# Loading the queries and keys of an attention head: three transfers of 128 partitions in place of six of 64

## The chip, the cores and the metric

The kernel runs on one core of a Trainium2 chip. A core has TensorE (PE in the profile; PEld is its weight load), VectorE (DVE), ScalarE (ACT), GpSimd (POOL) and SyncE (SP), which here does nothing but issue transfers. Transfers are issued from three queues, those of SP, ACT and POOL, and carried by sixteen DMA engines which the three queues share. The metric is device microseconds of one execution. Before the change it is 2463.16 us, the median of three runs from 2460.84 to 2463.77.

## The reference

One layer of a decoder, 2048 tokens of width 1024, all in float32. The change touches the attention branch:

```python
hn = _rmsnorm(h, ln_mix[i]); z = hn @ w_in[i]
q, k, v = ...                       # 8 heads of 64 channels, q scaled by 1/8
att = _dilated_attention(q, k, v, slopes)     # three window/dilation patterns per head, mixed
h = h + concat([att, pool]) @ w_out[i]
# then a gated MLP with a causal convolution, a gated per-layer embedding, a final RMSNorm
```

A pattern with window w and dilation d lets token t attend to t, t-d, ..., t-w. The kernel computes two score tiles for a block of 128 queries, a "near" one (the dense window) and a "far" one (both dilated windows), each with its own bias table, maximum and sum.

## The kernel before, in words

Every float32 product is made of TensorE products on a number's high part (rounded to the format `float32r`) and its low part (the rest). Projections, for instance, are three matmuls (`mm3`, L88). Attention scores do this differently: the contraction over 64 channels would fill only half of the 128 partitions. So `load_qk` (L502) lays a head out with its two parts stacked. `ks` has the high part of the keys on partitions 0 to 63 and the low part on 64 to 127. `qhh` has the high part of the queries twice, on both halves, and `qll` their low part twice. One matmul of `qhh` with `ks` then gives high times high plus high times low, and one of `qll` with `ks` adds the rest.

The kernel goes through three phases:

- `phase_project` (L170) works in token chunks. For each it computes queries, keys, values and the pooling input, splits them, and stores the parts to DRAM: queries in `g.qh` and `g.ql`, keys in `g.kh` and `g.kl` (L376 and L377), one tensor for each pair of heads, 128 channels by 2048 tokens. Values go to `g.vn` and `g.vf` (L391), pooling results to `g.mh` and `g.ml` (L463, L464). In the last chunk keys come before values, and the values' stores are issued from POOL.
- `phase_attention` (L486) runs over 128 steps, 16 blocks of queries for each of 8 heads. The order of PE, ACT, DVE and POOL in a step is written out by hand in `CFG["ord"]`; the order on SP's queue is set by the planner that schedules the program. Head 0's transfers are issued before the first step. Those of head h+1 are put in a list at step 1 of head h and one is taken from it at each step; SP sends it as soon as its tile is free. The tiles of a head come in two sets, of even and odd heads (`tag=f"qhh{e}"`, `bufs=1`), so the loads of head h+1 must wait until head h-1 has finished its scores, and no longer. The two bias tables `fb` and `nb` follow in the same list. The values `v` of a pair of heads are loaded by eight transfers, at fixed steps (`V_STEPS`). Every second head the statistics of a pair go through DRAM (`std`, `stf` on ACT's queue, `wd` on POOL's), come back as weights spread over 128 partitions (`wb`, L891), and POOL mixes near and far results and stores them in `g.mh`, `g.ml` (L924, L925).
- `phase_rest` (L930) has the output projection, the MLP and the rest.

The transfer of L891 is used below. It reads two rows of 512 numbers and writes each of them to 64 partitions:

```python
q.dma_start(w, g.wd[pr][2 * a : 2 * a + 2, None, cs].to_broadcast([2, DH, CH]))
```

A transfer's source and destination are nested lists of sizes. For the loads of 64 partitions both begin with 64; for L891 the source begins with 2, the destination with 128.

Of the kernel before, what the change touches and what calls it, by code (L numbers as in the profile page):

```python
# [11 lines left out]
F32R = mybir.dt.float32r  # L12
# [5 lines left out]
P = 128  # L18
D = 1024
KD = D // P  # L20
S = 2048
H = 8
DH = 64
# [31 lines left out]
def rdma(nc, dst, src):  # L55
    nc.sync.dma_start(fp(dst) if dst.dtype == F32R else dst, fp(src) if src.dtype == F32R else src)
# [113 lines left out]
def phase_project(tc, g, xT, w_in, pool_w, rcnt):  # L170
# [4 lines left out]
    with ExitStack() as ctx:  # L175
# [116 lines left out]
        for c, (t0, n) in enumerate(chunks):  # L292
            cs = slice(t0, t0 + n)
            final = c == len(chunks) - 1
            nxt = None
            for gi, grp in enumerate((0, 1, 2, 3) if not final else (0, 1, 3, 2)):
                if gi == 2 and not final:
                    tk.later(2, lambda st=nxt: scale(st))
                    tk.later(5, lambda st=nxt: spread_(st))
                nt = 4 if grp != 2 else n // P  # L300
                ps = [psum.tile([P, CH], F32, tag="b1", name=f"z{c}_{grp}_{j}") for j in range(nt)]
                apart = final and grp == 2
                for k in range(KD if not apart else 0):
                    if gi == 0 and c == 0 and k < KD - ACFG["nk"]:
                        norm_b(cur, k + ACFG["nk"])
                        cur.low()
                    ahead(step + ACFG["la"])
                    step += 1
                    wh, wl = held[grp, k]
                    ah, al = cur.hn[k]  # L310
                    for j in range(nt):
                        js = slice(j * P, (j + 1) * P)
                        if grp == 2:
                            mm3(nc, ps[j], ah[:, js], al[:, js], wh, wl, k == 0, k == KD - 1)
                        else:
                            mm3(nc, ps[j][:, :n], wh[:, js], wl[:, js], ah, al, k == 0, k == KD - 1)
                    tk.tick()
                    if gi == 0 and k == 6 and not final:
                        nxt = loads(c + 1)
                    if gi == 1 and not final:  # L320
                        square(nxt, k)
                    if gi == 3 and not final:
                        if k > 1:
                            nxt.low()
                        norm_a(nxt, k)
                        if k > 0:
                            norm_b(nxt, k - 1)
                    if gi == 0 and c == 0:
                        if k < 4:
                            square(cur, 2 * k)  # L330
                            square(cur, 2 * k + 1)
                        if k == ACFG["sc"]:
                            scale(cur)
                        if k == KD - 1:
                            spread_(cur)
                            inv = nxt.xs[0][:, n : 2 * n]
                            nc.scalar.copy(inv, cur.inv)
                    if gi == 0 and c > 0 and k < 2:
                        cur.low()
                        if k == 0:  # L340
                            norm_b(cur, KD - 1)
                    if c == 0 and gi == 0 and k == 4:
                        raw = small("pw_raw")
                        nc.sync.dma_start(raw.rearrange("p (a b) -> p a b", a=4), pool_w)
                        split(nc, pw_h.rearrange("p a b -> p (a b)"), pw_l.rearrange("p a b -> p (a b)"), raw)
                        nc.sync.dma_start(rc, rcnt)
                unscaled = list(range(nt)) if c == 0 and grp != 2 else []

                def by_inv():
                    if unscaled:  # L350
                        pu = ps[unscaled.pop(0)][:, :n]
                        nc.vector.tensor_tensor(pu, pu, inv, op=ALU.mult)

                by_inv()
                for j in range(nt):
                    if apart:
                        for k in range(KD):
                            js = slice(j * P, (j + 1) * P)
                            ah, al = cur.hn[k]
                            mm3(nc, ps[j], ah[:, js], al[:, js], *held[grp, k], k == 0, k == KD - 1)  # L360
                            if k % 4 == 3:
                                tk.tick()
                    by_inv()
                    pj = ps[j][:, :n]
                    pr = pj.rearrange("p (j r) -> p r j", r=4)
                    if grp == 0:
                        hi, lo = zpair("q", n)
                        nc.scalar.activation(hi, pj, AF.Copy, scale=QSCALE)
                        nc.vector.scalar_tensor_tensor(lo, pj, QSCALE, fp(hi), op0=ALU.mult, op1=ALU.subtract)
                        rdma(nc, g.qh[j][:, cs], hi)  # L370
                        rdma(nc, g.ql[j][:, cs], lo)
                    elif grp == 1:
                        hi, lo = (by_residue(z) for z in zpair("k", n))
                        nc.scalar.copy(hi, pr)
                        nc.vector.tensor_tensor(lo, pr, fp(hi), op=ALU.subtract)
                        rdma(nc, residues(g.kh[j], t0, n), hi)  # L376
                        rdma(nc, residues(g.kl[j], t0, n), lo)  # L377
                    elif grp == 2:
                        vt = sb.tile([P, H, 2, DH], F32R, tag="vt", bufs=NV, name="vt")
                        pv = ps[j].rearrange("p (h d) -> p h d", h=H)  # L380
                        if c == 0:
                            sc = cur.pw[:, j : j + 1]
                            nc.scalar.activation(vt[:, :, 0, :], pv, AF.Copy, scale=sc)
                            nc.vector.scalar_tensor_tensor(
                                vt[:, :, 1, :], pv, sc, fp(vt[:, :, 0, :]), op0=ALU.mult, op1=ALU.subtract
                            )
                        else:
                            nc.scalar.copy(vt[:, :, 0, :], pv)
                            nc.vector.tensor_tensor(vt[:, :, 1, :], pv, fp(vt[:, :, 0, :]), op=ALU.subtract)
                        for dst in (g.vn[t0 // P + j], g.vf[:, t0 // P + j]):  # L390
                            (nc.gpsimd if final else nc.sync).dma_start(  # L391
                                fp(dst.rearrange("r j h a d -> j r (h a d)")), fp(vt.rearrange("p h a d -> p (h a d)"))
                            )
                    else:
                        pool_branch(nc, g, sb, psum1, c, j, pj, t0, n, tails[j], rc, pw_h, pw_l, zpair, final)
            cur = nxt
# [7 lines left out]
def residues(t, t0, n):  # L404

    c, j0 = t0 // CH, t0 % CH // 4
    return t[:, c, :, j0 : j0 + n // 4]
# [78 lines left out]
def phase_attention(tc, g, mx, near_b, far_b):  # L486
# [5 lines left out]
    with ExitStack() as ctx:  # L492
# [8 lines left out]
        def load_qk(h):  # L501
            t = heads[h] = Shared()  # L502
            pr, e = h // 2, h % 2
            rows = slice(DH * e, DH * e + DH)
            t.qhh = sb.tile([P, S], F32R, tag=f"qhh{e}", bufs=1, name=f"qhh{h}")
            t.qll = sb.tile([P, S], F32R, tag=f"qll{e}", bufs=1, name=f"qll{h}")
            t.qr = t.qhh.rearrange("p (c r) -> p r c", r=4)
            t.qlr = t.qll.rearrange("p (c r) -> p r c", r=4)
            t.ks = sb.tile([P, NCH, 4, P], F32R, tag=f"ks{e}", bufs=1, name=f"ks{h}")
            t.nb = sb.tile([P, 256], F32, tag=f"nb{e}", bufs=1, name=f"nb{h}")  # L510
            t.fb = sb.tile([P, 512], F32, tag=f"fb{e}", bufs=1, name=f"fb{h}")
            loads = []
            for half in range(2):
                hs = slice(half * DH, half * DH + DH)
                loads.append((t.qhh[hs], g.qh[pr][rows]))
                loads.append((t.ks[hs], (g.kh if half == 0 else g.kl)[pr][rows]))
                loads.append((t.qll[hs], g.ql[pr][rows]))
            loads += [(t.fb, far_b[h]), (t.nb, near_b[h])]
            return loads

        near_v = g.vn.rearrange("n r j (p h) a d -> (r j) n p (h a d)", h=2)
        far_v = g.vf.rearrange("r (b m) j (p h) a d -> r (m j) b p (h a d)", m=4, h=2)
# [1322 lines left out]
def tile_layer(ctx, tc, xT, pT, vec, w_in, pool_w, w_out, w_up, w_down, w_gate, w_ple, near_b, far_b, rcnt, outT, upto=9):  # L1845
# [23 lines left out]

    g.qh = per(NPAIR, [P, S], F32R, "qh")  # L1870
    g.ql = per(NPAIR, [P, S], F32R, "ql")
    g.kh = per(NPAIR, [P, NCH, 4, P], F32R, "kh")
    g.kl = per(NPAIR, [P, NCH, 4, P], F32R, "kl")

    g.vn = dr.tile([NQ, 4, P // 4, H, 2, DH], F32R, tag="vn", name="vn")
    g.vf = dr.tile([4, NQ, P // 4, H, 2, DH], F32R, tag="vf", name="vf")
# [95 lines left out]
```

## Time and profile before

| | |
|---|---|
| median of the runs | 2463.16 us |
| span of the profiled execution (its own time is not on the page) | 2454.4 us |
| what lies outside the span, if that execution took the median | 8.8 us |
| TensorE busy | 2345.7 us, 96% of the span |
| attention, from its first score matmul to its last | 397.7 to 706.4 us |
| transfers issued at L56 for `qhh` and `qll`, `ks` | 16 and 16, 16 |
| median time of one such transfer from issue to landing | 10.7, 14.1 and 12.0 us |

"Idle" behind a group of instructions is the time for which the engine stood still just before them, and the name behind the arrow is what ended it. Times to landing run from the issue to the last of a transfer's bytes, so they hold what is queued ahead of it. GB/s in a stretch of time is what all sixteen DMA engines moved together.

### The profile page before, as it was taken

How to read it: one execution, taken by the hardware profiler on the slowest of the kernel's cores; microseconds unless marked ns; L12 is line 12 of the kernel's file. 1: busy time of each engine (PE TensorE's matmuls, PEld its weight loads, DVE VectorE, ACT ScalarE, POOL GpSimd, SP SyncE). 2: the span in 40 equal slices, each digit the busy share in tenths (PEclk: the TensorE clock that was granted, in tenths of full speed). 3: DMA queues.
4: the chain of work that ended last, by engine and by line, in shares of the span. 5: the costliest groups of instructions: out<-in, count | busy, mean ns of one | idle time of the engine just before them, and what ended most of it. 6: DMA issues, size and time to landing. Idle time of an engine off the chain costs nothing.

```text
span 2454.4 us, 32544 instructions
## 1 busy us (share of the span) xinstructions
PE 2345.7 (96%) x11251; PEld 1970.6 (80%) x11251; DVE 1723.2 (70%) x2705; ACT 1146.1 (47%) x2055; POOL 547.3 (22%) x552
## 2 busy tenths in 40 slices
PE   8999999888879999999999999999999999999998
PEld 7888887787767887888888787788878888888888
DVE  6645437787774367999999989877766565755655
ACT  5423326787761125445445545444445444543332
POOL 3312221044340023344332366100020000000100
PEclk9999999898989999999999999999999999999999
DMA  7535448878747576456566778544388676654332
GB/s 240 175 133 185 146 153 249 178 173 193 181 142 260 189 253 202 161 187 211 192 197 219 260 275 272 197 145 142 125 287 287 226 255 206 215 176 158 125 100 91
DMA packets 248516, 476.06 MB, mean 194 GB/s; under 512 B 47744, under 2 KB 74176, under 8 KB 245280
## 3 DMA queue, kind: packets, MB, share of 16 engines
q1 hardware_dynamic: 199376, 385.20, 49.7%
q0 software_dynamic: 29328, 61.02, 7.4%
q10 hardware_dynamic: 19648, 27.77, 3.3%
q8 instruction: 88, 1.44, 0.3%
q14 instruction: 76, 0.62, 0.1%
HBM read 313.08 MB, written 160.73 MB: 193 GB/s over the span
## 4 chain that ended last, share of the span: by engine, by line
PE 73%; DVE 10%; DMA 7%; issue 4%; ACT 2%; POOL 0%; DVEq 0%; POOLq 0%; ACTq 0%; SPq 0%
PE ua L1319 15%; PE uc L1319 8%; PE dn L90 5%; PE dn L89 5%; PE dn L91 5%; PE ub L1319 4%; PE z L91 4%; PE z L89 4%; PE z L90 4%; PE o L89 2%; PE o L91 2%; PE o L90 2%; PE gp L89 2%; PE gp L90 2%; PE gp L91 2%
## 5 line engine op out<-in xcount | busy, mean ns | idle before, releaser
L90 PE MATMUL dn<-al,wu 128*128 128x512 f32 x616 | 240.1, 390 | 4.7 <-DVE al L85 4.7
L89 PE MATMUL dn<-ah,wu 128*128 128x512 f32 x616 | 240.1, 390 | 0.0
L91 PE MATMUL dn<-ah,wu 128*128 128x512 f32 x616 | 239.8, 389 | 0.0
L85 DVE TENSOR_TENSOR al<-ra,ah 128x512 fp32r<-128x512 f32 x154 | 105.8, 689 | 114.1 <-ACT ah L84 110.7
L89 PE MATMUL z<-hnh,wh 128*128 128x512 f32 (+1 forms) x480 | 169.9, 354 | 9.5 <-ACT hnh L252 6.0
L90 PE MATMUL z<-hnl,wh 128*128 128x512 f32 (+1 forms) x480 | 169.7, 354 | 3.4 <-DVE hnl L253 3.3
L91 PE MATMUL z<-hnh,wl 128*128 128x512 f32 (+1 forms) x480 | 169.6, 353 | 2.3 <-POOL wl L85 1.7
L84 ACT CAST ah<-ra 128x512 fp32r<-128x512 f32 x154 | 95.2, 621 | 148.2 <-PE dn L91 130.6
L90 PEld LDWEIGHTS dn<-al,wu 128*128 128x128 f32 x616 | 115.6, 188 | 30.0 <-DVE al L85 6.2
L85 DVE TENSOR_TENSOR wu<-ru,wu 128x1024 fp32r<-128x1024 f32 x88 | 136.5, 1551 | 2.4 <-ACT wu L84 2.4
L89 PEld LDWEIGHTS dn<-ah,wu 128*128 128x128 f32 x616 | 115.6, 188 | 24.3 <-ACT ah L84 0.2
L91 PEld LDWEIGHTS dn<-ah,wu 128*128 128x128 f32 x616 | 115.6, 188 | 23.9
L1319 PE MATMUL uc<-a22h,wu 128*128 128x512 f32 x352 | 116.9, 393 | 3.4 <-DVE uv L1342 3.4
L1319 PE MATMUL ua<-s1h,wu 128*128 128x512 f32 x352 | 115.8, 390 | 3.0 <-ACT ug L1546 3.0
L1319 PE MATMUL ub<-a12h,wu 128*128 128x512 f32 x352 | 117.0, 393 | 0.7 <-ACT a12h L1375 0.6
L1319 PE MATMUL ua<-s2h,wu 128*128 128x512 f32 x352 | 115.9, 390 | 0.9 <-ACT ug L1520 0.7
L1319 PE MATMUL ua<-s4h,wu 128*128 128x512 f32 x352 | 115.7, 389 | 0.5 <-ACT uv L1567 0.5
L1319 PE MATMUL uc<-s3h,wu 128*128 128x512 f32 x352 | 115.6, 389 | 0.0
L1319 PE MATMUL ua<-a11h,wu 128*128 128x512 f32 x352 | 115.5, 389 | 0.0
L85 DVE TENSOR_TENSOR wu<-rw,wu 128x512 fp32r<-128x512 f32 x149 | 101.0, 687 | 17.3 <-ACT wu L84 17.3
L89 PEld LDWEIGHTS z<-hnh,wh 128*128 128x128 f32 x480 | 94.0, 196 | 21.5 <-ACT hnh L252 6.0
L155 DVE TENSOR_TENSOR acc<-acc,sq 128x512 f32<-128x512 f32 (+1 forms) x125 | 81.1, 649 | 42.0 <-ACT sq L154 28.5
(336 smaller groups left out, 6670.3 us busy)
## 6 DMA issues: line engine op xcount, KB each, us to landing
ru<-in_w_up_dram SPq DMA_DIRECT2D x66, 512.0 KB, 4.1
wr<-in_w_in_dram SPq DMA_DIRECT2D x64, 256.0 KB, 4.2
rw<-in_w_down_dram SPq DMA_DIRECT2D x61, 256.0 KB, 4.0
nt<-h SPq DMA_DIRECT2D x56, 256.0 KB, 3.8
td<-t SPq DMA_DIRECT2D x22, 512.0 KB, 2.6
t<-td SPq DMA_DIRECT2D x22, 512.0 KB, 3.7
nt<-in_w_down_dram POOLq DMA_DIRECT2D x44, 256.0 KB, 5.4
ra<-oq0s SPq DMA_DIRECT2D x44, 256.0 KB, 3.9
```

Of the source, the lines that this page charges most:

```text
L84: nc.scalar.copy(hi, src)
L85: (low or nc.gpsimd).tensor_tensor(lo, src, fp(hi), op=ALU.subtract)
L89: nc.tensor.matmul(ps, wh, ah, start=first, stop=False, skip_group_check=again)
L90: nc.tensor.matmul(ps, wh, al, start=False, stop=False, skip_group_check=again)
L91: nc.tensor.matmul(ps, wl, ah, start=False, stop=last, skip_group_check=again)
L155: nc.vector.tensor_tensor(acc[:, :n], acc[:, :n], sq[:, :n], op=ALU.add)
L1319: nc.tensor.matmul(pst, x[:, ksl], y, start=first and k == 0 and n == 0, stop=k == HK - 1 and n == 2, skip_group_check=True)
```

## The change

The high and low parts of the keys of a pair are put in one DRAM tensor, `g.kk`, with a leading size of 2, so that a head's keys can be fetched by one transfer to 128 partitions. The queries are still stored once; a transfer to 128 partitions reads them twice, through a leading size of 2 with a step of zero. A head takes three transfers of 1 MB in place of six of 512 KB. The rows are 8 KB each, as before, and the bytes are the same.

```diff
-                        rdma(nc, residues(g.kh[j], t0, n), hi)
-                        rdma(nc, residues(g.kl[j], t0, n), lo)
+                        rdma(nc, residues(g.kk[j][0], t0, n), hi)
+                        rdma(nc, residues(g.kk[j][1], t0, n), lo)
...
-            loads = []
-            for half in range(2):
-                hs = slice(half * DH, half * DH + DH)
-                loads.append((t.qhh[hs], g.qh[pr][rows]))
-                loads.append((t.ks[hs], (g.kh if half == 0 else g.kl)[pr][rows]))
-                loads.append((t.qll[hs], g.ql[pr][rows]))
-            loads += [(t.fb, far_b[h]), (t.nb, near_b[h])]
-            return loads
+            both = lambda z: z[pr][None, rows].to_broadcast([2, DH, S])
+            return [
+                (t.qhh, both(g.qh)),
+                (t.ks.rearrange("p c r j -> p (c r j)"), g.kk[pr][:, rows].rearrange("a p c r j -> a p (c r j)")),
+                (t.qll, both(g.ql)),
+                (t.fb, far_b[h]),
+                (t.nb, near_b[h]),
+            ]
...
-    g.kh = per(NPAIR, [P, NCH, 4, P], F32R, "kh")
-    g.kl = per(NPAIR, [P, NCH, 4, P], F32R, "kl")
+    g.kk = per(NPAIR, [2, P, NCH, 4, P], F32R, "kk")
```

## The prediction

> **What bounds the kernel now.** I read the page first, then the eight heads of the attention as stretches of time, then what PE, ACT and DVE wait for there.
>
> ```profile
> span 2454.4 us, 32544 instructions
> PE 2345.7 (96%) x11251; PEld 1970.6 (80%) x11251; DVE 1723.2 (70%) x2705; ACT 1146.1 (47%) x2055; POOL 547.3 (22%) x552
> ```
>
> ```profile
> 397.80:433.50 35.70, 28.90 (x177) 26.13 (x175) 27.22 (x87) 30.15 (x85) 2.21 (x4) 0.94 1.00 279
> 433.50:470.10 36.60, 33.58 (x206) 30.41 (x206) 29.82 (x88) 30.60 (x85) 0.00 (x0) 0.92 0.66 149
> 470.10:512.20 42.10, 34.37 (x212) 31.12 (x212) 32.29 (x99) 32.45 (x90) 4.28 (x6) 0.92 0.74 169
> 512.20:546.80 34.60, 31.44 (x207) 28.69 (x206) 30.18 (x89) 31.93 (x89) 20.70 (x21) 1.00 0.88 207
> 546.80:594.80 48.00, 37.06 (x212) 33.13 (x212) 32.22 (x99) 32.43 (x90) 16.39 (x19) 0.86 0.76 181
> 594.80:629.40 34.60, 31.44 (x207) 28.68 (x206) 30.19 (x89) 31.93 (x89) 20.98 (x22) 1.00 0.93 214
> 629.40:673.60 44.20, 35.52 (x212) 31.75 (x212) 32.22 (x99) 32.45 (x90) 14.59 (x17) 0.92 0.73 177
> 673.60:707.40 33.80, 30.63 (x200) 27.87 (x200) 29.38 (x87) 31.12 (x87) 30.30 (x31) 1.00 0.37 133
> ```
>
> A row is a head; its edges are the starts of every sixteenth score matmul. Behind the length stand the busy times of PE, PEld, DVE, ACT and POOL, then clock, DMA share and GB/s. A head takes 34 to 48 us, and PE, ACT and DVE are each busy for some 30 of them: a chain that passes through all three sets the pace. The last two numbers matter here: the loads of the next head go on beneath this work. The waits of the three engines in these 310 us that end with a transfer are few:
>
> ```profile
> ACT ev L659 <- DMA v<-vn: 7.6, 2, 5.0
> ACT ev L659 <- DMA stf<-sy: 3.2, 1, 3.2
> DVE tt L577 <- PE sf L562: 4.7, 1, 4.7
> DVE lo L862 <- DMA sf<-stf: 4.7, 2, 2.5
> PE sn L573 <- DMA qll<-ql: 2.6, 1, 2.6
> ```
>
> The third is put down to PE, but it is the first use of head 1's bias table, which had just landed. Together 22.8 us: all that faster loads could give back here.
>
> **How fast the loads are, and what else the trace shows.**
>
> ```profile
> L56 SPq DMA_DIRECT2D qhh<-qh x16: 450/481/1232, 358.2 to 636.5; - x16
> DMA to landing us min/median/max: 4.7/10.7/17.0
> L891 POOL DMA_DIRECT2D wb<-wd x24: 787/830/852, 503.2 to 689.3; - x24
> DMA to landing us min/median/max: 7.5/9.5/24.4
> ```
>
> ```profile
> mh<-mh POOLq DMA_DIRECT2D x4, 256.0 KB, 2.7
> ```
>
> ```profile
> 364.00:376.00 12.00, 12.00 (x55) 9.93 (x54) 2.09 (x3) 3.38 (x6) 1.90 (x5) 1.00 1.01 204
> 411.00:417.00 6.00, 5.55 (x40) 5.23 (x39) 5.63 (x17) 5.71 (x18) 0.00 (x0) 1.00 1.11 376
> 505.00:506.60 1.60, 1.51 (x10) 1.51 (x11) 1.51 (x5) 1.35 (x5) 0.60 (x1) 1.00 0.33 54
> 508.80:510.40 1.60, 1.24 (x8) 0.92 (x7) 1.58 (x4) 1.59 (x4) 0.00 (x0) 1.00 0.40 149
> ```
>
> Four stretches in which one kind of load runs alone. From 364 us, head 0's loads of 64 partitions: 204 GB/s. From 411 us, loads of `v` to 128 partitions: 376. So half the partitions go at half the rate, and the change should double it. But from 505 us the first `wb` is alone in flight, also a write to 128 partitions: 54 GB/s, a seventh. From 508.8 us three of them: 149, so no memory limit holds one at 54; it is the single transfer that is narrow. Its best landing is 7.5 us, where 256 KB of `mh` on the same queue take 2.7. What sets `wb` apart is its source, whose outermost size is 2. 376 GB/s over sixteen engines are 23.5 each; 54 is what two of them move. I read it so: a transfer is dealt out by its outermost size, and two outer pieces occupy two engines. The new loads of `qhh`, `qll` and `ks` all begin with 2 on the source side.
>
> The Trainium skill, DMA: Bandwidth & Descriptors, section Rules for kernel authors, has this rule: the engine count follows from the slowest size of both patterns, and a leading broadcast of c copies keeps a transfer on at most c engines. It names no exception for SP's queue. By it each new load gets 2 of 16; the `wb` rows agree with it, though no run here shows it on SP's queue.
>
> **Removed.** Per head, three issues on SP of about 0.5 us (481 ns in the row of `qhh`), 24 in all, 12 us of SP's time. Nothing waits for SP's own time here; the loads are hidden beneath a head of 34 us or more. Value zero; bounds: the few us of a load that lands that much earlier.
>
> **Moved.** The stores of the keys keep their number, size and queue. They now share a tensor in pairs, in disjoint pieces. Should each wait for its neighbour, the weight loads behind them on SP would be late. The stores of `vn` and `vf` (L391) already go piecewise into one tensor each, and SP's waits at them from 20 to 350 us all end with compute:
>
> ```profile
> SPq L391 <- DVE vt L389: 27.5, 3, 10.7
> SPq L391 <- DVE x L244: 2.9, 3, 1.2
> SPq L391 <- DVE vt L384: 1.1, 1, 1.1
> ```
>
> So zero; the upper bound is one landing, 2.9 us in the row of `vn` below, for each of five chunks.
>
> **Added: the narrow loads.** One load is 1.049 MB. At 54 GB/s that is 19.4 us, at a third of 149, 21.1. I take 52: 20.2 us, and since all three go through SP's queue I put them on the same two engines, one behind the other: 60.5 us (58.3 to 63.5). Other transfers pass these two engines too, each with a sixteenth of its bytes, at 26 GB/s. On SP's queue they stand in line; those of POOL share with it.
>
> ```profile
> q0 software_dynamic: 1792, 6.29, 34.0%
> vn<-vt POOLq DMA_DIRECT2D x4, 512.0 KB, 2.9
> ```
>
> ```profile
> v<-vf SPq DMA_DIRECT2D x12, 512.0 KB, 9.5
> v<-vn SPq DMA_DIRECT2D x11, 512.0 KB, 9.6
> wb<-wd POOLq DMA_DIRECT2D x20, 256.0 KB, 10.4
> mh<-ah POOLq DMA_DIRECT2D x8, 256.0 KB, 10.6
> ml<-al POOLq DMA_DIRECT2D x8, 256.0 KB, 11.2
> fb<-in_far_b_dram SPq DMA_DIRECT2D x6, 256.0 KB, 15.4
> nb<-in_near_b_dram SPq DMA_DIRECT2D x6, 128.0 KB, 11.6
> ```
>
> The first is POOL's queue from 358 to 404 us, 6.29 MB of value and pooling stores: 6.29 / 16 / 0.026 = 15 us on each engine. The second lists the transfers from head 1's start to head 7's, beside the loads in question: 23 x 0.524 + 36 x 0.262 + 6 x 0.262 + 6 x 0.131 = 23.9 MB, 57 us on each engine, 9.6 per head (5.8 if POOL's do not delay).
>
> Now the sum, head by head:
> - Head 0: issued at 358.2, first bytes some 3.5 us later (4.7 us to the earliest landing, less its data), then 60.5 and 15: start at 437, not 397.8 (low 420, without the stores).
> - Head 1: its loads are already issued; on SP's queue eight `v` and two bias tables stand before them, 4.6 MB, 11 us. 437 + 11 + 60.5 = 508.5, not 433.5.
> - Heads 2 to 7: a load may be issued when the head before last has done its scores, some 35 us after that head began. That is before the previous loads end, so the two engines never run dry and each head takes 60.5 + 9.6 = 70.1 us, for 36 us of work. Head 7 starts at 508.5 + 6 x 70.1 = 929, not 673.6.
>
> PE meets the wait at L572 and L573, and everything behind it on PE, then DVE and ACT, stands still. The values `v` land behind one to three loads, but are used from six steps into a head on, and the waits within heads 2, 4 and 6 fall inside the 70 us. From head 7 on nothing changes. So +255 us: 2463.2 + 255 = 2718. The span would be 2710; the 8.8 us around it stay. Low end: 58.3, 5.8 and 420 give 874 for head 7, +200, 2663. High end: 63.5, and 3.5 us lost at each head, give 514 + 6 x 76.6 = 974, +300, 2764.
>
> **Rivals.**
> - *The doubling comes (not slower).* 54 GB/s may belong to POOL's queue or to 64 reads of one row, not to the outer 2; then SP's loads use sixteen engines and 376 GB/s. Loads of a head take 8.4 us, not 15.4. For it: only `wb` shows 54. Against: `mh` on POOL's queue is fast, and three `wb` reach 149. Of the 22.8 us of waits about half go, since `sf` and `stf` also pass the same busy engines: 2463 - 11 = 2452, between 2441 and 2463. It decides as soon as more than about four engines carry a load (3 x 1.049 MB in 30 us are 105 GB/s). The same page's rule on two transfers to disjoint partition halves, to use one of 128 partitions instead, speaks for it; the 204 and 376 above agree, and by it alone the time would be this one.
> - *Two engines each, but not the same two.* The three `wb` at 149 GB/s were on three pairs. If SP's loads also spread, they take 20 us side by side, plus 9.6 and 3.5: 33, just within a head. Head 1 would start about 4 us late, the ten other engines make the statistics quicker by as much: 2463, from 2455 to 2475. For it: those three. Against it: they are dealt out by POOL's own queue; no row of SP's queue bears on it, and I take dealing out by turns to be the less likely. The same page's section Why a DMA increments its semaphore by 16 and not by 1 says that SP's kind of queue takes the lowest-numbered engines each time, which no row here shows.
> - *Sixteen engines, but hidden anyway.* The waits come from latency, and nothing moves: 2463, within 4.
>
> **How the numbers follow.** Two shared engines 0.82, the doubling 0.08, different pairs 0.08, hidden 0.02. A measurement here can tell 0.2%, 5 us, from no change. Faster: most of the doubling and a little of the pairs, 0.08. Same: 0.08. Slower: 0.84, with part of the pairs. The likeliest's own bounds are 2663 to 2764; since it must carry nearly all of the 8 in 10, and the share of other traffic is the least certain term, I widen to 2620 and 2810.
>
> **What would show it.** After the change: a DMA share near 2/16 and some 52 GB/s through most of the attention; landings of `qhh`, `ks`, `qll` above 20 us; heads of about 70 us in the stretches; PE's longest waits at L572 and L573, ended by these loads; PE busy unchanged near 2346 us in a span of 2710. Wrong if their rate is near 376 GB/s (first rival), or if three land together after 20 us each (second). If heads are as long as 80 us, other traffic was undercounted; if the loads of a head begin only after the head before has ended, the running ahead was.

## The result and the profile after

After the change the kernel takes 2741.14 us (median of four runs, 2737.94 to 2742.97). The kernel before, run beside it, takes 2462.0 us (four runs, 2460.66 to 2463.77). The ratio is 1.1121, with a 95% interval from 1.1103 to 1.114: slower by 279 us. The forecast was 2718 us, its range 2620 to 2810.

From the page of the changed kernel: the span, the busy times, the granted clock and the DMA share in 40 slices of 68 us, and the costliest group that waits for a transfer.

```profile
span 2738.5 us, 32503 instructions
PE 2365.0 (86%) x11251; PEld 1983.8 (72%) x11251; DVE 1720.8 (63%) x2705; ACT 1146.9 (42%) x2055; POOL 545.8 (20%) x552
PEclk9999996768677789999999999999999999999999
DMA  7544343123333246674555667774437867674332
L573 PE MATMUL sn<-ks,qll 128*128 128x256 f32 (+1 forms) x128 | 40.9, 319 | 169.1 <-DMA qll<-ql 169.1
```

The span is 284 us longer and PE's work has grown by only 19 us, so the rest is standing still. In the slices of the attention the DMA share falls to one to three tenths. The last row names the longest wait for a transfer: PE waited 169 us for `qll` ahead of the matmuls of L573. PE's 19 us are not more instructions (their count is the same); nearly all of them lie in the eight heads below, where the digits of the clock fall to between 6 and 8.

The eight heads as stretches of time, with the columns of the prediction's table:

```profile
438.60:510.40 71.80, 29.83 (x175) 26.52 (x175) 25.98 (x82) 29.36 (x84) 0.00 (x0) 0.69 0.27 94
510.40:575.60 65.20, 34.39 (x206) 30.78 (x206) 29.96 (x88) 31.98 (x88) 0.00 (x0) 0.76 0.23 78
575.60:652.50 76.90, 38.92 (x211) 34.23 (x211) 32.16 (x98) 32.75 (x89) 5.24 (x6) 0.72 0.29 92
652.50:726.30 73.80, 34.09 (x206) 30.47 (x206) 29.96 (x88) 31.98 (x88) 30.24 (x31) 0.73 0.33 113
726.30:803.50 77.20, 38.36 (x211) 33.77 (x211) 32.35 (x98) 32.54 (x89) 5.26 (x6) 0.74 0.29 94
803.50:878.70 75.20, 34.87 (x206) 31.25 (x206) 29.97 (x88) 32.08 (x88) 30.27 (x31) 0.73 0.33 114
878.70:957.00 78.30, 37.45 (x211) 32.88 (x211) 32.32 (x98) 32.67 (x89) 5.26 (x6) 0.72 0.28 89
957.00:995.30 38.30, 33.67 (x199) 30.48 (x200) 29.04 (x86) 29.94 (x82) 30.44 (x31) 0.87 0.34 117
```

A head holds the same 30 us of work for ACT and DVE as before and takes 65 to 78 us. The last head, for which nothing more is loaded beneath it, takes 38.3. Head 7 starts at 957.0 in place of 673.6, and these 283.4 us are all of the longer span.

Two stretches with nothing but the new loads in flight, the first while head 0 is loaded, the second in head 1:

```profile
364.00:376.00 12.00, 12.00 (x55) 9.93 (x54) 2.09 (x3) 3.49 (x6) 2.38 (x6) 1.00 0.13 53
520.00:545.00 25.00, 22.64 (x150) 20.54 (x149) 21.84 (x64) 23.01 (x64) 0.00 (x0) 1.00 0.13 54
```

A DMA share of 0.13 is two engines of sixteen. In the first stretch all three loads of head 0 have been issued (at 359.5, 360.3 and 360.9 us), and together they still move 53 GB/s on two engines. Had each taken a pair of its own, it would be six engines and some 160 (three times 53, an estimate). The trace's records of single packets agree: the three end one after the other, at 381.7, 409.0 and 437.5 us. They also show what this does to others. A wide load ends with sixteen writes of 4 bytes, a narrow one with two. While head 0's third load moves, the bias table `nb` and the first two loads of `v`, all wide, get 14 of these each (from 411.0, 432.3 and 434.4 us on); the last two do not come before 436.8. So a wide transfer behind a narrow one waits for its shares on two engines.

Waits from 397 to 996 us: engine, tile and line, what ended the wait, us in total, times, the longest.

```profile
ACT ee L589 <- DVE st L577: 255.2, 43, 40.8
PE sn L573 <- DMA qll<-ql: 169.1, 8, 28.0
DVE tt L577 <- DMA nb<-in_near_b_dram: 134.8, 5, 41.5
PE sn L572 <- DMA ks<-kk: 53.9, 4, 21.2
ACT ev L659 <- DMA v<-vf: 50.1, 3, 18.1
```

PE waits at L573 in every head. ACT's 255 us are the same stall one engine further on. The table `nb`, last in the list of a head, comes later still in five heads, and the values `v` hold ACT once in each of heads 2, 4 and 6.

### The profile page after: what moved, and what is told of

Same layout as the page of the kernel before. It is cut to its first block, busy times and chain, and to the rows that moved or that the text cites. A ratio compares the mean times of both kernels' runs of the same rounds, so it can differ in the third digit from the quotient of the medians.

```text
span 2738.5 us, 32503 instructions
## 1 busy us (share of the span) xinstructions
PE 2365.0 (86%) x11251; PEld 1983.8 (72%) x11251; DVE 1720.8 (63%) x2705; ACT 1146.9 (42%) x2055; POOL 545.8 (20%) x552
## 4 chain that ended last, share of the span: by engine, by line
PE 66%; DMA 13%; DVE 6%; another core or an unknown queue 5%; issue 3%; ACT 2%; SPq 2%; POOL 0%; POOLq 0%; DVEq 0%; ACTq 0%
PE ua L1319 14%; PE uc L1319 7%; PE dn L89 5%; PE dn L90 5%; PE dn L91 5%; DMA nb<-in_near_b_dram 4%; PE ub L1319 4%; PE z L91 3%; PE z L89 3%; PE z L90 3%; DMA v<-vf 2%; PE o L89 2%; PE o L91 2%; PE o L90 2%
## 5 line engine op out<-in xcount | busy, mean ns | idle before, releaser
L573 PE MATMUL sn<-ks,qll 128*128 128x256 f32 (+1 forms) x128 | 40.9, 319 | 169.1 <-DMA qll<-ql 169.1
L589 ACT ACTIVATE ee<-tt,st 128x256 f32<-128x256 f32 (+1 forms) x128 | 64.4, 503 | 256.2 <-DVE st L577 255.2
L577 DVE CUSTOM_DVE_ANT_0 tt<-sn,nb 128x256 f32<-128x256 f32 (+1 forms) x128 | 53.1, 415 | 172.5 <-DMA nb<-in_near_b_dram 134.8
L573 PEld LDWEIGHTS sn<-ks,qll 128*128 128x128 f32 x128 | 27.7, 217 | 171.2 <-DMA qll<-ql 171.2
```

The source lines that it names most:

```text
L573: nc.tensor.matmul(st.nv, t.qll[:, qs], keys, start=False, stop=True, skip_group_check=True)
L577: nc.vector.tensor_tensor_reduce(st.tt[:, st.ns], st.nv, st.t.nb[:, 256 - st.wn :], 1.0, BIG, ALU.add, ALU.min, st.nm1)
L589: nc.scalar.activation(st.ee[:, st.ns], st.tt[:, st.ns], AF.Exp, bias=st.nm1, scale=-1.0, accum_out=st.d1)
```

## The experiments

The comparisons are with runs of the kernel before on the same chip, whose medians were 2459 to 2464 us.

**The same loads with the row outermost** (`e1_row_outermost`). Three loads of 128 partitions as in the change, the same bytes and the same shared tensor. Only the two sizes are exchanged (for the keys in the DRAM tensor as well), so that the source begins with 64 rows and holds the two copies (or the high and the low part) inside. Row d lands on partitions 2d and 2d+1 for queries and keys alike, which the contraction does not mind.

```diff
-  both = lambda z: z[pr][None, rows].to_broadcast([2, DH, S])
+  both = lambda z: z[pr][rows, None].to_broadcast([DH, 2, S])
-  g.kk[pr][:, rows].rearrange("a p c r j -> a p (c r j)")
+  g.kk[pr][rows].rearrange("p a c r j -> (p a) (c r j)")
-  g.kk = per(NPAIR, [2, P, NCH, 4, P], F32R, "kk")      # stores to kk[j][0], kk[j][1]
+  g.kk = per(NPAIR, [P, 2, NCH, 4, P], F32R, "kk")      # stores to kk[j][:, 0], kk[j][:, 1]
```

> The changed kernel with its two source sizes exchanged: the row of a channel is outermost (64), the two parts or copies of it come inside. A head is still three transfers of 1 MB to 128 partitions from one tensor of keys; only the order of the channels on the partitions differs, for queries and keys alike. Theory (a transfer is dealt out to as many DMA engines as its outermost size allows, and the change left two): sixteen engines again, at least 204 and up to 376 GB/s while head 0 is loaded, 2441 to 2463 us, most likely 2452. Rival 1 (the price lies in the 128 partitions, the 1 MB or the repeated reading of a row): still about 53 GB/s and about 2741 us. Rival 2 (it lies in the shared tensor of the keys): about 2741 us.

Measured: 2433.36 us (2428.11 to 2436.81), ratio 0.988 (0.9861 to 0.9899). It is faster than both kernels, by 1.2% against the one before, and below the 2441 us that I had set as the least. While head 0 is loaded, and in heads 1, 2, 4 and 6, its stretches read:

```profile
364.00:370.00 6.00, 6.00 (x28) 4.99 (x27) 0.00 (x0) 0.62 (x1) 2.73 (x5) 1.00 0.98 406
...
431.90:466.40 34.50, 31.36 (x207) 28.61 (x206) 30.09 (x89) 31.82 (x89) 0.00 (x0) 1.00 0.40 149
466.40:503.90 37.50, 32.26 (x212) 29.09 (x211) 32.24 (x99) 32.33 (x90) 3.79 (x5) 1.00 0.55 190
...
538.50:576.80 38.30, 32.21 (x212) 29.03 (x211) 32.21 (x99) 32.31 (x90) 10.25 (x13) 1.00 0.62 209
...
611.30:652.20 40.90, 33.75 (x213) 30.54 (x212) 32.37 (x99) 32.54 (x90) 10.56 (x13) 0.96 0.55 185
```

The three loads, with the first of a bias table behind them, move 406 GB/s on all sixteen engines, where the changed kernel moved 53 on two. Nothing but the order of the two sizes differs, and with it the order of the keys in DRAM and of the channels on the partitions. So the loss belongs to that order, and not to fewer transfers, to 128 partitions or to the shared tensor. Most of the doubling of the rate is there for the taking: 217 GB/s before in the same six microseconds, 406 here. It is worth more than I expected: heads 2, 4 and 6 took 42.1, 48.0 and 44.2 us before and take 37.5, 38.3 and 40.9 here.

**Two, four or eight as the outermost size of the old loads** (`e5_outer_2`, `e5_outer_4`, `e5_outer_8`). The kernel before, its six loads of 64 partitions kept. Only the order in which a load goes through its 64 rows is written with an outermost size o, here 4. Rows change places in queries and keys alike.

```diff
-  loads.append((t.qhh[hs], g.qh[pr][rows]))
+  loads.append((t.qhh[hs], g.qh[pr][rows].rearrange("(i o) s -> o i s", o=4)))
   # the same for ks and qll
```

> The kernel before the change, with its six transfers of 64 partitions, no repeated reading and separate tensors; only the order in which the 64 rows of a transfer are taken is changed, as two interleaved sets of 32, so that the source begins with 2. Theory: two engines, 53 GB/s while head 0 is loaded, and the time of the changed kernel, 2741 us (2715 to 2770), although nothing of the change but the outermost size is in it. Rival 1: as before, 2462 us. Rival 2: 2462 us.

> The same with four interleaved sets of 16 rows. Theory: four engines, 107 GB/s while head 0 is loaded; a head's loads then take 30 us and with the other traffic 40 to 44, a little over the 36 to 40 that a head lasts now: 2475 to 2510 us. Rival (the interleaved order itself is slow, whatever the number of sets): as with two sets.

> The same with eight interleaved sets of 8 rows. Theory: eight engines at 26 GB/s each make 208 GB/s, which is the 204 that sixteen engines reach with these transfers of 64 partitions: no change, 2462 us within 5. Rival (the interleaved order itself is slow): far above 2500 us.

| outermost size | time, us | ratio (95%) | DMA share, 364 to 370 us | GB/s |
|---|---|---|---|---|
| 64 (before) | 2462 | 1 | 1.03 | 217 |
| 8 | 2490.04 | 1.0107 (1.0087 to 1.0127) | 0.64 | 158 |
| 4 | 2534.13 | 1.028 (1.0248 to 1.0312) | 0.26 | 72 |
| 2 | 2755.45 | 1.1213 (1.1174 to 1.1252) | 0.12 | 31 |

The row of each while head 0 is loaded: first the kernel before, then size 8 (with a second stretch, without the bias tables that run in the first), then 4, then 2 (with a later stretch):

```profile
364.00:370.00 6.00, 6.00 (x29) 4.95 (x28) 0.00 (x0) 0.51 (x1) 1.70 (x4) 1.00 1.03 217
```

```profile
364.00:370.00 6.00, 6.00 (x28) 4.99 (x27) 0.00 (x0) 1.25 (x2) 3.14 (x3) 1.00 0.64 158
370.00:376.00 6.00, 6.00 (x28) 4.96 (x27) 0.88 (x2) 1.42 (x3) 0.48 (x4) 1.00 0.50 115
```

```profile
364.00:370.00 6.00, 6.00 (x28) 4.99 (x27) 0.00 (x0) 0.62 (x1) 2.26 (x5) 1.00 0.26 72
```

```profile
364.00:370.00 6.00, 6.00 (x28) 4.97 (x27) 0.00 (x0) 0.62 (x1) 2.35 (x5) 1.00 0.12 31
376.00:379.00 3.00, 3.00 (x15) 2.46 (x14) 0.00 (x0) 0.00 (x0) 0.00 (x0) 1.00 0.12 52
```

The shares, 0.50, 0.26 and 0.12, are 8, 4 and 2 engines of 16. So the count of engines follows the outermost size step by step, in transfers of 64 partitions too, and without any repeated reading of a row. The records of packets agree: a load ends with 2, 4 and 8 writes of 4 bytes, and with 16 in `e1`. Size 2 by itself brings the whole loss of the change.

The times of sizes 8 and 4 lie above the ranges expected (2457 to 2467 and 2475 to 2510). I had taken the limit of 204 GB/s for the transfers of 64 partitions as one on their sum, which eight engines would still reach. They reach 115, which is 14 GB/s on each, as in the kernel before (217 / 16 = 14). With sizes 4 and 2 it is 72 / 4 = 18 and 31 / 2 = 16 at first, against 53 / 2 = 27 in the changed kernel. So the expected rates of 107 and 53 were missed as well, but the slowness does not stay: with size 2 the rate rises to 52 within the same loads, when a load to the other half of the partitions has been issued as well. That alone is not the condition, for with size 8 all six loads had been issued by 366.3 us and the rate from 370 us is still 14 on each engine. Why it rises, no run here settles; whether it matters which partitions are written at the same moment was not tried.

**One part of the change alone.** `e2_keys_alone` loads the keys by one narrow transfer and leaves the queries as four of 64 partitions. `e3_queries_alone` loads the queries by two narrow transfers and the keys by two of 64. `e4_shared_tensor_alone` has the six old loads, from the shared tensor.

```diff
 # the lists of loads, shortened; lo_ and hi_ are partitions 0 to 63 and 64 to 127
 e2:  (t.qhh[lo_], g.qh[pr][rows]), (t.ks, g.kk[pr][:, rows]), (t.qll[lo_], g.ql[pr][rows]),
      (t.qhh[hi_], g.qh[pr][rows]), (t.qll[hi_], g.ql[pr][rows])
 e3:  (t.qhh, both(g.qh)), (t.ks[:DH], g.kk[pr][0][rows]), (t.qll, both(g.ql)), (t.ks[DH:], g.kk[pr][1][rows])
 e4:  loads.append((t.ks[hs], g.kk[pr][half][rows]))        # the rest as before
```

> One part of the change alone: the keys come by one transfer of 128 partitions with the outermost size 2, the queries by four of 64 as before. Theory (bytes on two engines): 20.2 us of narrow load per head, 5 for the two engines' share of the queries, 9.6 of other traffic and the 4.3 by which heads were longer than reckoned: 39 us, beside the 36 to 40 a head lasts now; head 0 and 1 about 4 us later, the short heads 4 us longer: 2475 us, between 2460 and 2490. Rival (the repeated reading of the queries carries the price): 2462. Rival (the shared tensor of the keys carries it): near 2741.

> The other part alone: the two transfers of the queries with the leading broadcast of 2, the keys by two of 64 partitions from the shared tensor. Theory: 40.4 us of narrow load, 2.5 for the share of the keys, 9.6 and 4.3: 57 us a head; head 0 starts 22 us later, head 1 40, head 7 140: 2603 us, between 2560 and 2620. Rival (the keys carry the price): 2462. Rival (the repeated reading carries all of it): near 2741.

> Only the shared tensor of the keys: stores into it as in the change, loads by six transfers of 64 partitions as before. Theory: no wait between the stores of the two parts, 2462 us within 5. Rival (each store waits for its neighbour in the tensor): up to 15 us more, and waits of SP at the stores of the keys that end with a transfer of the keys.

| | time, us | ratio (95%) |
|---|---|---|
| keys alone | 2523.83 | 1.0271 (1.0248 to 1.0295) |
| queries alone | 2629.04 | 1.0689 (1.0669 to 1.0709) |
| shared tensor alone | 2462.75 | 1.0008 (0.9994 to 1.0021) |

The shared tensor costs nothing, as forecast. One narrow load per head costs 63 us, two cost 169 and three 279. Both parts cost more than their ranges allowed (up to 2490 and 2620 us), the first by far: I had reckoned that 20 us on two engines lie beneath a head of 35, and that only what passes the same two engines would be late. Below are waits in the attention of the kernel with the keys alone (its lines stand two lower than before) and the stretch of its head 0. The last two rows are SP's wait for the stores of the values, in this kernel and in the one before.

```profile
PE sn L574 <- DMA qhh<-qh: 37.8, 3, 22.9
DVE lo L864 <- DMA sf<-stf: 35.5, 3, 12.9
DVE tt L579 <- DMA nb<-in_near_b_dram: 24.9, 1, 24.9
```

```profile
400.60:460.50 59.90, 29.49 (x176) 26.99 (x175) 27.41 (x87) 30.36 (x85) 2.22 (x4) 0.77 0.60 182
```

```profile
SPq L56 <- DMA vf<-vt: 38.5, 1, 38.5
```

```profile
SPq L56 <- DMA vf<-vt: 39.2, 1, 39.2
```

These waits are ended not by the narrow load but by wide transfers: queries, bias tables and statistics. They have shares on the two busy engines, as `nb` and `v` above, and none has landed before its last share has. Where landings can be read, they agree: the loads of `v`, wide in both kernels, land after 14.6 us in the median, 8.5 before. How much of the 63 us each of them brings is not shown.

Head 0 shows it most: it lasts 59.9 us, 35.7 before, because head 1's loads are late. SP's wait for the stores of the values is no longer than before, but it ends 8 us later; the loads of `v` are then issued from 410.7 us (from 402.5 before), and head 1's queries and keys behind them from 419.4 (from 410.3), when head 0 has been running for 19 us.

**The bias tables first** (`e6_tables_first`). In the changed kernel DVE waits 134.8 us for `nb`. Is it late by its place at the end of the list?

```diff
 # sources left out
-  return [(t.qhh, ..), (t.ks, ..), (t.qll, ..), (t.fb, far_b[h]), (t.nb, near_b[h])]
+  return [(t.fb, far_b[h]), (t.nb, near_b[h]), (t.qhh, ..), (t.ks, ..), (t.qll, ..)]
```

> The changed kernel with the two bias tables of a head listed ahead of its three loads instead of behind. Theory (bytes on two engines; the tables are under 1 us of a head on each): 2736 us, between 2728 and 2742. Rival (SP is held at issues of up to 43 us, and this makes the tables late and costs the 4 us a head by which the forecast was short): about 2715 us.

Measured: 2745.14 us (2743.51 to 2749.13), ratio 1.1166 (1.1147 to 1.1186): no gain, and 0.4% above the changed kernel's ratio if anything. The same view of waits:

```profile
PE sn L573 <- DMA qll<-ql: 130.5, 8, 28.2
DVE tt L577 <- PE sn L573: 124.4, 57, 40.5
```

DVE now waits the same 120 to 135 us for PE instead of for `nb`. So its place in the list does not make the time; the two engines have the same bytes to move, in whatever order.

**What else passes the two engines** (`e8_after_wb_halves`, `e7_wb_halves`). In the changed kernel heads 2, 4 and 6 take some 12 us more than head 1. In their last third, POOL's `wb` transfers run, which occupy two engines each. If these were the two of SP, `wb` would be what I undercounted. The edit makes each `wb` two transfers of 64 partitions whose source begins with the 64 copies. `e8` is the changed kernel with it, `e7` the kernel with the row outermost.

```diff
-  q.dma_start(w, g.wd[pr][2 * a : 2 * a + 2, None, cs].to_broadcast([2, DH, CH]))
+  for e in range(2):
+      q.dma_start(w[e * DH : e * DH + DH], g.wd[pr][2 * a + e : 2 * a + e + 1, cs].to_broadcast([DH, CH]))
```

> The changed kernel, with each fetch of the mix's weights (wb, L891) made two transfers of 64 partitions whose source begins with the 64 copies, so that each is dealt over sixteen engines. In the changed kernel heads 2, 4 and 6 take 76.9, 77.2 and 78.3 us and head 1 takes 65.2, though by their other bytes they should take some 5 us more than head 1, not 12. Theory: in their last third four wb transfers, each on two engines itself, come to lie on the very pair that the loads use. Then heads 2, 4 and 6 fall by 5 to 8 us each and the time to 2715 to 2728. Rival: POOL's queue deals its transfers out by turns, wb puts no more on the pair than on any other engine, and the extra time of these heads comes from SP being held at its issues; then heads and time stay, 2735 to 2747, or rise by the twelve more issues of POOL.

> The kernel with the rows outermost (e1_row_outermost, 2433), with the same edit of wb as e8_after_wb_halves. The fetches of wb reach all engines and land sooner than the 9.4 us median there, and POOL waits less than 25 us for them between heads 2 and 7. POOL's mix is off the path that sets a head, so the theory expects no gain: 2428 to 2438. If wb's narrow transfers hold up the statistics or the loads on their two engines, a few us more go: 2418 to 2428. If 48 issues in place of 24 of 0.84 us make POOL late, 2438 to 2450.

Measured: `e8` 2742.28 us (2738.88 to 2744.23), ratio 1.1141 (1.112 to 1.1162): no gain. `e7` 2427.08 us (2424.94 to 2431.22), ratio 0.9865 (0.9846 to 0.9884). Heads 1 and 2 of `e8`, and the landing of `wb`, first in `e8`, then in `e7` with its issues:

```profile
511.80:576.80 65.00, 34.47 (x206) 30.87 (x206) 29.97 (x88) 31.97 (x88) 0.00 (x0) 0.76 0.23 78
576.80:653.10 76.30, 38.54 (x211) 33.95 (x211) 32.32 (x98) 32.78 (x89) 19.00 (x25) 0.72 0.33 104
```

```profile
DMA to landing us min/median/max: 6.7/8.9/13.3
```

```profile
L892 POOL DMA_DIRECT2D wb<-wd x48: 522/532/557, 494.7 to 661.3; - x48
DMA to landing us min/median/max: 2.7/3.8/10.4
```

In `e8`, `wb` lands after 8.9 us in place of 22.5, yet head 2 is as long as it was (76.3 and 76.9), so `wb` on SP's pair is not what makes head 2 long. The same transfers, dealt over all engines in both kernels, land after 3.8 us without narrow loads beside them (`e7`) and after 8.9 with them (`e8`). In `e7` the rule bears fruit at a second place: the landing falls from 9.4 us in `e1` to 3.8, an issue costs POOL 0.53 us in place of 0.84, and its waits for `wb` in the attention, 25.1 us in `e1`, are gone. Whether this moves the time is not shown: the intervals of `e1` and `e7` overlap, and the 8 us between their profiled spans (2433.3 and 2425.1) are no more than the spread of runs of one kernel. At 2427 us it is in any case faster than the kernel before.

## Why the prediction was right

- **Two engines, in one line.** Right, and shown: share 0.13 and 53 GB/s with three loads in flight, the shares of 8, 4 and 2 engines by outermost size, and 406 GB/s once the row is outermost. The Trainium skill, DMA: Bandwidth & Descriptors, section Rules for kernel authors, whose rule I weighed against the `wb` rows, holds on SP's queue as well. That the same two engines are taken each time, which its section Why a DMA increments its semaphore by 16 and not by 1 states for SP's kind of queue, agrees with the 53 GB/s of three loads, and the rival of different pairs falls with it. The trace does not name the engines, but head 0's three loads, in flight together, end one after the other (at 381.7, 409.0 and 437.5 us), which loads on three pairs would not. That POOL's transfers go round by turns, as the section has it too, agrees with `e8`.
- **Head 0 and head 1.** Forecast 437 and 508.5, measured 438.6 and 510.4. By the trace's records of packets head 0's three loads move from 361.5 to 437.5 us, 76.0 us for 60.5 + 15; then 11.7 us pass for 11, and head 1's loads take 60.9 for 60.5. So these terms held. One was off: the first bytes come 2.0 us after the issue, not 3.5, and it is luck that the issue came 1.3 us later than in the kernel before.
- **The heads after.** Forecast 70.1 us a head, measured (957.0 - 510.4) / 6 = 74.4. This is the mis-sized term: 26 us by head 7. It was not the bytes. GB/s times length over heads 1 to 6 gives 43.3 MB; less six times 3.15 MB of narrow loads, 24.4 MB are other traffic, where I had 23.9. What failed, for half of it, was "the two engines never run dry". SP's issues during head 5, up to the start of head 6, with their start and length:

```profile
803.46 0.51 SPq L56 DMA_DIRECT2D qhh<-qh  x1
804.06 2.45 SPq L56 DMA_DIRECT2D ks<-kk  x1
806.56 21.05 SPq L56 DMA_DIRECT2D qll<-ql  x1
827.70 5.27 SPq L56 DMA_DIRECT2D fb<-in_far_b_dram  x1
833.02 21.33 SPq L56 DMA_DIRECT2D nb<-in_near_b_dram  x1
854.44 14.73 SPq L56 DMA_DIRECT2D v<-vf  x2
869.27 7.48 SPq L56 DMA_DIRECT2D v<-vn  x1
876.84 1.13 SPq L56 DMA_DIRECT2D qhh<-qh  x1
```

  SP is held inside an issue for up to 21 us here while the two engines work off what they have. The issues behind stand still, and `qhh` of head 7 is issued only at 876.8, 1.9 us before head 6 starts. I had said some 35 us into the head before last. That holds for the tile, for head 5's last score matmul starts 38 us into it, at 841.4, but not for SP's turn. The records of packets show no narrow load moving from 877.9 to 881.1, and five such gaps from head 2 to head 6 make 13.5 us. The other 12 us or so are open: the three loads of a head take 72.0 us on average from their first packet to their last, not 70.1. The third load of heads 3, 5 and 7, which moves in the last part of heads 2, 4 and 6, is the slowest, at 35 to 36 GB/s; `e8` took away the cause that I suspected.
- **The base.** In every run since, what lies outside the span is 1.7 to 3.1 us, not 8.8: the execution profiled before, with its span of 2454.4, was not one of the runs shown, but a quicker one. In spans the forecast missed by 2738.5 - 2710 = 28.5 us, in time by 23: this hid some 5 us of the miss.
- **What it would show.** PE's waits at L572 and L573 came as forecast. A DMA share of 0.13 and 53 GB/s show only where the new loads are alone; a whole head has 0.23 to 0.34 and 78 to 114 GB/s, for the other traffic runs beside them. PE's busy time did not stay at 2346: it rose to 2365 with the lower clock, at no cost that the waits show, since PE waits for loads. The profile gives no landings for the new loads, nor for the other loads of SP in these heads, but the first load's packets move for 20.2 us, the 20.2 of the sum. And the hold shows in the issues: `qll`, which took SP 0.6 us before, takes 18.8 in the median:

```profile
L56 SPq DMA_DIRECT2D qll<-ql x8: 2052/18822/21048, 360.8 to 895.4; - x8
```

- **"All that faster loads could give back", 22.8 us.** About right, and I priced too little of it: with the row outermost the eight heads together take 285.5 us in place of 309.6, 24 less. I had given the doubling 11 us, half of the waits. The medians differ by 30 and the profiled spans by 21, because the profiled execution of the kernel before was a quick one.

## What to carry to other kernels

Merging two half transfers into one of 128 partitions paid here only where the merged pattern still began with a large size: a leading 2, whether it is a repeat with step zero or a real dimension, put each load on two engines of sixteen and cost 279 us in all, and the same loads with the row first gained 30. Read the DMA share of a stretch in which one transfer runs alone: 0.13 is two engines, whatever the transfer was meant to do. And a narrow transfer is no private matter: one narrow load of 20 us beneath a head of 35 still cost 63 us over eight heads, because every wide transfer has a piece on the same two engines and lands with the slowest.

## What the runs showed of the hardware that was not expected

- SP does not merely put a transfer in line: with two engines full, it stays in the issue, 18.8 us in the median for `qll` and 43.5 us for head 0's `fb`, and holds all later issues. From 520 to 545 us, within two such holds, the DMA share is 0.13.
- Transfers to 64 partitions ran at some 14 GB/s on each engine with 16 and with 8 engines, so with 8 it was no limit on their sum that held them. With an outermost size of 2 the rate began at 31 GB/s on two engines and rose to 52; the condition is open.
- In the waiting heads the granted clock was 0.69 to 0.76, and 0.86 to 1.00 before. It was 1.00 in the stretch from 520 to 545 us, in which head 1 works without waiting, so I read the low clock as a result of the standing still, not as its cause.
